# A three-group feed-forward stage: the first group's down products plain, the down weights' Strassen operands made in the second group

## The chip, the cores and the metric

One core of one Trainium2 chip. The metric is the device time of one execution, in microseconds (us), the median of several runs. The engines are TensorE (PE, with its weight loads as PEld), VectorE (DVE), ScalarE (ACT), GpSimd (POOL) and SyncE (SP, which here only issues DMAs). Each engine works through its own instructions in the order in which they were queued and waits on semaphores for the others.

## What is computed

One decoder layer for 2048 prompt tokens, 16 meta tokens and 8 x 4 sample tokens of width 1024: a mixer of three head groups, then a dense SwiGLU feed-forward network with hidden width 2816, then a norm. The change touches the feed-forward network alone:

```python
def _swiglu(hn, w_ffn_in, w_ffn_out):
    g, u = jnp.split(hn @ w_ffn_in, 2, axis=-1)
    return (jax.nn.silu(g) * u) @ w_ffn_out
...
        h = h + _swiglu(_rmsnorm(h, norm_ffn[l]), w_ffn_in[l], w_ffn_out[l])
...
    return _rmsnorm(h, norm_final), stacked
```

The outputs are float32. The kernel multiplies in float16, with each operand split into a high and a low half and three passes for each product (high x high, high x low, low x high; `PASSES`).

## The kernel before

The mixers fill the first 1034 us and are not touched. The feed-forward network then runs over three groups of token tiles, here called group 0, 1 and 2: the first two hold six tiles of 128 tokens, the last four tiles and the short tile 0. Tokens are paired, so that the matmuls of a group run over 384, 384 and 280 columns.

**Strassen.** Both products are made with seven products of blocks instead of eight (Winograd's form). For that each operand is needed as seven blocks: some as they are, four as sums. For a weight tile, `left` (gate and up weights, L1015 to L1018) and `right` (down weights, L1022 to L1025) make the four sums on POOL, and `operands` splits plain blocks and sums into high and low halves: ACT rounds to float16 (L155), DVE takes the rest (L156), in three pieces of 512, 256 and 1024 columns a tile.

**Hidden.** For each of 11 units `jq` of 256 hidden columns, `hidden` calls `quad` twice, for gate and up. Each `quad` makes seven products of 12 matmuls (L1239), combined on ACT, DVE and POOL; the POOL combinations L1248 and L1249 stand in the middle, and DVE's products with silu (L1262) need them. `put` then writes the down products' operands `hh`, high half by ACT (L1268) and low half by DVE (L1269): three blocks as they are, and four sums, which POOL makes first (L1274 to L1280).

**Down.** The units are taken in four parts of 2, 3, 3 and 3 (`PARTS`). After a part's hidden units, `down` runs for each half `m` of the output columns and each pair of tiles: seven products of 3 matmuls a unit with 256 columns (L1292), each summed over the part's units in PSUM, then combined and added to the residual rows `xr` (two ACT, eight DVE and three POOL instructions, L1302 to L1330).

**Weights.** Group 0 loads the raw weights (`raw`, six buffers), makes the operands of 44 gate and up tiles and 22 down tiles, and stores each tile of 896 KB in scratch memory (`kept`, tiles `w`, six buffers). Groups 1 and 2 load them back into eleven `w` buffers of a new pool, which is opened once, when group 1 begins. In parts 1 and 2 of group 0, `prep_late` also prepares x operands of later tiles, in the same buffers. Loads and stores are issued by SP in program order; the tile framework lets each wait for the last user of its buffer, and instructions of one engine stand in the order that the framework's scheduler gave them.

Of the kernel before, what the change touches and what calls it, by code (L numbers as in the profile page):

```python
# [17 lines left out]
P = 128  # L18
# [41 lines left out]
def trunk(ctx, tc, I, O, groups):  # L60
# [1049 lines left out]

    pg_cm = tc.tile_pool(name="pg", bufs=1, side="left", reuse_waits="tile")
    pg = [pg_cm.__enter__()]
    w_bufs = [6]

    def raw_tile():
        return pg[0].tile([P, 4, 256], F32, tag="raw", bufs=6, name=nm("raw"))

    def w_full():
        return pg[0].tile([P, 2, 7, 256], F16, tag="w", bufs=w_bufs[0], name=nm("w"))

    def w_tile():
        w = w_full()
# [2 lines left out]
    def sum_tile():  # L1125
        return pg[0].tile([P, 4, 256], F32, tag="sums", bufs=2, name=nm("sums"))

    def kept(dram, make):

        w = w_full()  # L1130
        parts = [w[:, 0], w[:, 1]]
        if w_bufs[0] == 6:
            make(parts)
            nc.sync.dma_start(dram, w.rearrange("p a o c -> p (a o c)"))
        else:
            nc.sync.dma_start(w.rearrange("p a o c -> p (a o c)"), dram)
        return parts
# [41 lines left out]
    def gu_operands(c0):  # L1179

        rows = w_gu[:, c0 : c0 + 256].rearrange("(h q k p) c -> q h p k c", h=2, q=2, p=P)

        def make(w, q):
            raw = raw_tile()
            for h in range(2):
                nc.sync.dma_start(raw[:, 2 * h : 2 * h + 2], rows[q, h])
            a = [[raw[:, 2 * h : 2 * h + 2, u * P : (u + 1) * P] for h in range(2)] for u in range(2)]
            left(w, sum_tile(), a[0][0], a[0][1], a[1][0], a[1][1], raw[:, :, 0:P], WG)

        return [kept(wgu_d[c0 % DFF // 256, c0 // DFF, q], lambda w: make(w, q)) for q in range(2)]  # L1190

    def dn_operands(jq, m):


        def make(w):
            raw = raw_tile()
            c = slice(m * 512, m * 512 + 512)
            nc.sync.dma_start(raw.rearrange("p (k h) c -> p k (h c)", k=2), w_dn[2 * jq * P : 2 * jq * P + 2 * P, c].rearrange("(k p) c -> p k c", p=P))
            right(w, sum_tile(), raw[:, 0], raw[:, 1], raw[:, 2], raw[:, 3], raw.rearrange("p (k h) c -> p h k c", k=2)[:, 0], WS)

        return kept(wdn_d[jq, m], make)

    gu_first = [gu_operands(c) for c in (0, DFF)]
    interleave(outs)
# [4 lines left out]
    with (  # L1209
# [45 lines left out]
        def hidden(q, jq, n):  # L1255
# [15 lines left out]
            put(A11, a11)  # L1271
            put(A12, a12)
            put(A22, a22)
            G.tensor_tensor(s1, a21, a22, op=ALU.add)  # L1274
            put(S1, s1)
            G.tensor_tensor(s2, s1, a11, op=ALU.subtract)
# [4 lines left out]
            put(S4, s4)  # L1281

        PRODS = ((A11, B11), (S2, T2), (S3, T3), (S1, T1), (A12, B21), (A22, T4), (S4, B22))

        def down(ws, x1, x2_, c, off, L):

# [57 lines left out]
        put_off = [pr for pr in all_pairs[early:] if pr[0]] + [[0]]  # L1344

        for gi, grp in enumerate(groups):
            if gi == 1:
                pg_cm.__exit__(None, None, None)
                pg_cm = tc.tile_pool(name="ph", bufs=1, side="left", reuse_waits="tile")
                pg[0] = pg_cm.__enter__()  # L1350
                w_bufs[0] = 11
            n = half[gi]

            rows2 = [[(pr[0], 0, P), (pr[1], 0, P)] if len(pr) == 2 else [(0, 0, T0 // 2), (0, T0 // 2, T0 // 2)] for pr in pairs(grp)]
# [6 lines left out]
            for q0, q1 in PARTS:  # L1361
# [8 lines left out]
                for m in range(2):  # L1370
                    c = slice(m * 512, m * 512 + 512)
                    ws = [dn_operands(jq, m) for jq in range(q0, q1)]
                    for ra, rb in rows2:
                        for _ in range(3):
                            next(ahead, None)
                        down(ws, xr[ra], xr[rb], c.start, offs[ra[0]][1], ra[2])
                        if final:
                            for rw in (ra, rb):
                                L = rw[2]
                                S.activation(ft2("junk", [P, D], F16)[:L, c], xr[rw][:L, c], AF.Square, accum_out=sq[rw][:L, m : m + 1])  # L1380
# [326 lines left out]
```

## Time and profile before

| what | value |
| --- | --- |
| median of 3 runs | 2410.7 us (2409.39 to 2413.79) |
| the profiled execution | 2401.93 us, its span 2399.9 us |
| mean granted clock of TensorE | 0.973 |
| group 0 on TensorE | 1034.64 to 1589.44 us of the span |
| group 1 | 1589.44 to 2043.36 us |
| group 2 and the end | 2043.36 to 2399.9 us |

The profiled execution lies 0.4% below the median. All views (windows, timeline, groups by line) are of this one execution, in us from the start of its span. Busy time of an engine that is off the critical path costs nothing in itself; what counts is which wait ends last before TensorE goes on.

### The profile page before, as it was taken

The numbers are of one execution on the slowest core, as the hardware profiler recorded it, in microseconds if no ns is written. First come the engines' busy times: TensorE is split into PE (matmuls) and PEld (weight loads), VectorE is DVE, ScalarE is ACT, GpSimd is POOL, SyncE is SP. The second block draws the span as 40 slices with busy tenths as digits, with TensorE's granted clock in tenths as the row PEclk, the third lists the DMA queues.
The fourth block names the chain that finished last, engine by engine and source line by source line (L and its number), as shares of the span: only waits on it lengthen the run. The fifth ranks groups of instructions, "written<-read, shape, count | busy, mean of one in ns | idle before, by whom it ended". The sixth has DMA issues, their size and how long they took to land. (4 is left out here: it accounts for less than half of the span.)

```text
span 2399.9 us, 51972 instructions
## 1 busy us (share of the span) xinstructions
PE 2215.4 (92%) x20298; PEld 1605.7 (67%) x20298; DVE 1673.4 (70%) x4064; ACT 941.8 (39%) x2526; POOL 1148.9 (48%) x1595
## 2 busy tenths in 40 slices
PE   6999999999999899787989979789999999999996
PEld 6677767767777445444657566567686867888886
DVE  8789888988988776558778687655454535655546
ACT  7455545545445432334343434422212122332323
POOL 7333233333333364559768787634332324544435
PEclk9999999999999999898999989999999999999998
DMA  7233333333323755995536545684334247744441
GB/s 259 46 67 70 67 74 62 75 65 80 66 65 83 188 192 181 304 305 193 188 140 216 190 169 203 178 305 174 123 121 157 108 168 194 272 176 172 181 166 39
DMA packets 294328, 364.95 MB, mean 152 GB/s; under 512 B 203807, under 2 KB 234479, under 8 KB 294066
## 3 DMA queue, kind: packets, MB, share of 16 engines
q1 hardware_dynamic: 285090, 331.02, 44.2%
q0 software_dynamic: 4384, 15.93, 1.7%
q10 hardware_dynamic: 4608, 14.68, 1.6%
q8 instruction: 159, 2.61, 0.4%
q14 instruction: 87, 0.71, 0.1%
HBM read 212.24 MB, written 103.50 MB: 132 GB/s over the span
## 5 line engine op out<-in xcount | busy, mean ns | idle before, releaser
L1239 PE MATMUL s<-x,w 128*128 128x384 f16 (+1 forms) x5544 | 827.8, 312 | 20.4 <-DMA w<-wgu_scratch 7.8
L1239 PEld LDWEIGHTS <-w 128*128 128x128 f16 x5544 | 543.2, 98 | 302.8 <-issue 19.0
L1292 PE MATMUL dn<-w,hh 128*128 128x256 f16 (+1 forms) x4158 | 446.6, 279 | 54.8 <-ACT hh L1268 21.8
L1292 PEld LDWEIGHTS <-hh 128*128 128x128 f16 (+1 forms) x4158 | 380.6, 99 | 119.6 <-issue 29.5
L212 PEld LDWEIGHTS <-xT 128*128 128x128 f16 (+1 forms) x1992 | 176.1, 99 | 188.6 <-issue 18.2
L1268 ACT ACTIVATE hh<-tmp 128x384 f16<-128x384 f32 (+1 forms) x231 | 112.4, 494 | 282.7 <-DVE tmp L1262 167.4
L1248 POOL TENSOR_TENSOR tmp<-tmp,tmp 128x384 f32<-128x384 f32 (+1 forms) x66 | 67.1, 1017 | 276.3 <-ACT tmp L1247 272.8
L1269 DVE TENSOR_TENSOR hh<-tmp,hh 128x384 f16<-128x384 f32 (+1 forms) x231 | 143.4, 628 | 75.7 <-ACT hh L1268 74.0
L212 PE MATMUL wo<-wo,xT 128*128 128x512 f16 x768 | 176.3, 387 | 7.6 <-DVE xn L992 3.0
L156 DVE SCALAR_TENSOR_TENSOR w<-raw,w 128x512 f16<-128x512 f32 (+1 forms) x136 | 108.5, 830 | 14.2 <-ACT w L155 14.2
L553 POOL TENSOR_TENSOR t<-t 128x8 f32<-128x8 f32 (+2 forms) x100 | 24.9, 249 | 188.2 <-DVE k L551 100.6
L1250 DVE TENSOR_TENSOR tmp<-s,tmp 128x384 f32<-128x384 f32 (+1 forms) x66 | 34.2, 519 | 108.4 <-PE s L1239 108.4
L212 PE MATMUL d<-xT,qf 128*128 128x128 f16 (+1 forms) x1632 | 107.4, 220 | 0.0
L156 DVE SCALAR_TENSOR_TENSOR w<-sums,w 128x1024 f16<-128x1024 f32 x68 | 98.5, 1450 | 9.5 <-ACT w L155 9.4
L1259 ACT ACTIVATE tmp<-tmp 128x384 f32<-128x384 f32 (+1 forms) x132 | 61.6, 490 | 109.0 <-DVE tmp L1250 51.7
L1324 DVE SCALAR_TENSOR_TENSOR xr<-dn,xr 128x256 f32<-128x256 f32 x192 | 78.9, 417 | 35.0 <-PE dn L1292 30.8
L212 PE MATMUL d<-xT,bqk 128*128 128x128 f16 (+1 forms) x1632 | 100.1, 220 | 3.3 <-DVE e L278 3.3
L212 PEld LDWEIGHTS <-qf 128*128 128x128 f16 x1632 | 95.2, 100 | 7.2 <-issue 2.1
L212 PEld LDWEIGHTS <-bqk 128*128 128x128 f16 x1632 | 93.0, 99 | 5.5 <-issue 4.6
L212 PE MATMUL d<-aig,xT 128*128 128x512 f16 (+1 forms) x408 | 92.7, 379 | 3.4 <-DVE g L358 3.4
L212 PE MATMUL d<-bvo,xT 128*128 128x512 f16 (+1 forms) x408 | 95.6, 380 | 0.2 <-DVE qlo L325 0.2
L212 PE MATMUL d<-xT,cq 128*128 128x128 f16 (+1 forms) x1632 | 94.8, 217 | 0.0
(536 smaller groups left out, 4044.2 us busy)
## 6 DMA issues: line engine op xcount, KB each, us to landing
w<-wgu_scratch SPq DMA_DIRECT2D x88, 896.0 KB
wgu_scratch<-w SPq DMA_DIRECT2D x44, 896.0 KB
w<-wdn_scratch SPq DMA_DIRECT2D x44, 896.0 KB
raw<-in_w_ffn_in_dram SPq DMA_DIRECT2D x88, 256.0 KB
wdn_scratch<-w SPq DMA_DIRECT2D x22, 896.0 KB
xs<-in_x_prompt_dram SPq DMA_DIRECT2D x26, 512.0 KB
x_scratch<-pT ACTq DMA_DIRECT2D x28, 448.0 KB
raw<-in_w_ffn_out_dram SPq DMA_DIRECT2D x22, 512.0 KB
```

What stands on the lines that cost most here:

```text
L156: V.scalar_tensor_tensor(lo, src, scale, hi, op0=ALU.mult, op1=ALU.subtract)
L212: T.matmul(out, lh(k, a), rh(k, b), start=(n == 0), stop=(n == 3 * nk - 1))
L553: G.tensor_tensor(tn, tv[:, :, :, 0], tv[:, :, :, 1], op=ALU.mult)
L1239: T.matmul(out, A[k // 2][p][:, a, k % 2 * P : k % 2 * P + P], x2[r][:, k // 2, op, k % 2, :n], start=i == 0, stop=i == 11)
L1248: G.tensor_tensor(r12, r12, r22, op=ALU.add)
L1250: V.tensor_tensor(r11, prod(A12, B21), r11, op=ALU.add)
L1259: S.activation(d, d, AF.Silu, scale=UF)
L1268: S.activation(hi, v, AF.Copy)
L1269: V.tensor_tensor(lo, v, hi, op=ALU.subtract)
L1292: T.matmul(out, hh[p][:, q, a, off : off + L], ws[q][r][:, b], start=(q, p, r) == order[0], stop=(q, p, r) == order[-1])
L1324: V.scalar_tensor_tensor(x[:L, cc], m, UD, x[:L, cc], op0=ALU.mult, op1=ALU.add)
```

## The change

Three things change. (1) In group 0 the down products are made plainly, by `down_plain`: from four blocks, each output block as six matmuls a unit (two halves k, three passes) with 512 columns, summed over the part's units, and one DVE instruction that adds the result to `xr`. `hidden` then puts four blocks of `hh` in place of seven, with the block A21 in the place of S1, and makes no sums. The down weights of group 0 are only split, one ACT and one DVE instruction of 1024 columns a tile. (2) The 22 down tiles' Strassen operands are made and stored by group 1 (the argument `when` of `kept`), which therefore loads raw down weights; group 2 loads the operands as before. (3) Each group now has a pool of its own: six raw and six w buffers in group 0, three and eight in group 1, eleven w buffers in group 2. `left`, `right`, `quad` and `down` are not altered.

```diff
-    w_bufs = [6]
+    stage, raw_bufs, w_bufs = [0], [6, 3], [6, 8, 11]
...
-    def kept(dram, make):
+    def kept(dram, make, when):
...
-        if w_bufs[0] == 6:
+        if stage[0] == when:
...
+        return [kept(wgu_d[c0 % DFF // 256, c0 // DFF, q], lambda w: make(w, q), 0) for q in range(2)]
...
-        return kept(wdn_d[jq, m], make)
+        if stage[0] == 0:
+            w = w_tile()
+            split_w(load().rearrange("p a c -> p (a c)"), *(z[:, 0:4].rearrange("p a c -> p (a c)") for z in w), WS)
+            return w
+        return kept(wdn_d[jq, m], make, 1)
...
             put(A22, a22)
+            if stage[0] == 0:
+                put(A21, a21)
+                return
...
+        def down_plain(ws, x1, x2_, c, off):
+
+            order = [(q, k, p, r) for q in range(len(ws)) for k in range(2) for p, r in PASSES]
+            for x, ops in ((x1, (A11, A12)), (x2_, (A21, A22))):
+                out = pbt("dn")
+                for o in order:
+                    q, k, p, r = o
+                    T.matmul(out, hh[p][:, q, ops[k], off : off + P], ws[q][r][:, 2 * k : 2 * k + 2].rearrange("p h c -> p (h c)"), start=o == order[0], stop=o == order[-1])
+                V.scalar_tensor_tensor(x[:, c : c + 512], out, UD, x[:, c : c + 512], op0=ALU.mult, op1=ALU.add)
...
-            if gi == 1:
+            if gi:
                 pg_cm.__exit__(None, None, None)
-                pg_cm = tc.tile_pool(name="ph", bufs=1, side="left", reuse_waits="tile")
+                pg_cm = tc.tile_pool(name=f"ph{gi}", bufs=1, side="left", reuse_waits="tile")
                 pg[0] = pg_cm.__enter__()
-                w_bufs[0] = 11
+                stage[0] = gi
...
-                        down(ws, xr[ra], xr[rb], c.start, offs[ra[0]][1], ra[2])
+                        if gi == 0:
+                            down_plain(ws, xr[ra], xr[rb], c.start, offs[ra[0]][1])
+                        else:
+                            down(ws, xr[ra], xr[rb], c.start, offs[ra[0]][1], ra[2])
```

How the order of instructions changes, at three places. First POOL ahead of the last hidden unit of group 0's last part. Before, the four-instruction sums of two down tiles (`sums` from `raw`) stand ahead of the last unit's up combination L1248:

```order
L1249 TENSOR_TENSOR tmp_21519<-tmp_21519,tmp_21518 128x384
L1022 TENSOR_TENSOR sums_22127<-raw_22125 128x256
L1024 TENSOR_TENSOR sums_22127<-raw_22125 128x256
L1023 TENSOR_TENSOR sums_22127<-raw_22125,sums_22127 128x256
L1022 TENSOR_TENSOR sums_22142<-raw_22140 128x256
L1024 TENSOR_TENSOR sums_22142<-raw_22140 128x256
L1025 TENSOR_TENSOR sums_22127<-raw_22125,sums_22127 128x256
L1023 TENSOR_TENSOR sums_22142<-raw_22140,sums_22142 128x256
L1025 TENSOR_TENSOR sums_22142<-raw_22140,sums_22142 128x256
L1248 TENSOR_TENSOR tmp_21657<-tmp_21657,tmp_21659 128x384
```

Now, in the same part (L1258 and L1259 are the former L1248 and L1249), the last gate and up sums stand ahead of the second of three units, and from there on the combinations follow each other:

```order
L1016 TENSOR_TENSOR sums_20592<-sums_20592,raw_20589 128x256
L1018 TENSOR_TENSOR sums_20592<-raw_20589,sums_20592 128x256
L1258 TENSOR_TENSOR tmp_20177<-tmp_20177,tmp_20179 128x384
L1259 TENSOR_TENSOR tmp_20179<-tmp_20179,tmp_20178 128x384
L1258 TENSOR_TENSOR tmp_20317<-tmp_20317,tmp_20319 128x384
L1259 TENSOR_TENSOR tmp_20319<-tmp_20319,tmp_20318 128x384
```

No sum stands ahead of the last unit there any more; in parts 1 and 3 of group 0, eight gate and up sums of the next part still do. The second place is POOL ahead of the last unit of group 1's second part. Before, the gate's and the up's combinations of a unit followed each other with no sums between:

```order
L1248 TENSOR_TENSOR tmp_23871<-tmp_23871,tmp_23873 128x384
L1249 TENSOR_TENSOR tmp_23873<-tmp_23873,tmp_23872 128x384
L1248 TENSOR_TENSOR tmp_23983<-tmp_23983,tmp_23985 128x384
L1249 TENSOR_TENSOR tmp_23985<-tmp_23985,tmp_23984 128x384
L1274 TENSOR_TENSOR tmp_23982<-tmp_23871,tmp_23873 128x384
```

Now the sums of two down tiles stand between them:

```order
L1259 TENSOR_TENSOR tmp_22521<-tmp_22521,tmp_22520 128x384
L1022 TENSOR_TENSOR sums_24097<-raw_24095 128x256
L1024 TENSOR_TENSOR sums_24097<-raw_24095 128x256
L1023 TENSOR_TENSOR sums_24097<-raw_24095,sums_24097 128x256
L1022 TENSOR_TENSOR sums_24112<-raw_24110 128x256
L1024 TENSOR_TENSOR sums_24112<-raw_24110 128x256
L1025 TENSOR_TENSOR sums_24097<-raw_24095,sums_24097 128x256
L1023 TENSOR_TENSOR sums_24112<-raw_24110,sums_24112 128x256
L1025 TENSOR_TENSOR sums_24112<-raw_24110,sums_24112 128x256
L1258 TENSOR_TENSOR tmp_22631<-tmp_22631,tmp_22633 128x384
```

The last unit's L1258 now follows eight sums. The third place is SP at the border between groups 1 and 2, where `w` are tiles of operands, `x` the group's inputs and `xr` its residual rows. Before, the first loads of group 2's gate weights follow the last down loads of group 1 and stand ahead of the inputs:

```order
L1136 DMA w_26920<-wdn_scratch 128x3584
L1136 DMA w_27250<-wgu_scratch 128x3584
L1136 DMA w_27252<-wgu_scratch 128x3584
L1136 DMA w_27362<-wgu_scratch 128x3584
L1057 DMA_TRANSPOSE x_2033_15774<-x_scratch 128x14x128
```

Now they follow group 1's last store, the inputs and the residual rows:

```order
L1057 DMA_TRANSPOSE x_2033_15774<-x_scratch 128x14x128 x2
L1068 DMA x_2032_15773<-x_scratch 128x28x24
L1068 DMA x_2033_15774<-x_scratch 128x28x24
L1392 DMA xr_26134<-h_scratch 24x1024
L1392 DMA xr_26132<-h_scratch 24x1024
L1138 DMA w_26136<-wgu_scratch 128x3584
L1138 DMA w_26138<-wgu_scratch 128x3584
```

The first load of group 2 belongs to the new pool and waits for the last down product of group 1.

More of the change, by code (lines that the diff above doesn't have):

```diff
@@ L1112, in trunk @@
     pg = [pg_cm.__enter__()]
-    w_bufs = [6]
+    stage, raw_bufs, w_bufs = [0], [6, 3], [6, 8, 11]
     def raw_tile():
-        return pg[0].tile([P, 4, 256], F32, tag="raw", bufs=6, name=nm("raw"))
+        return pg[0].tile([P, 4, 256], F32, tag="raw", bufs=raw_bufs[stage[0]], name=nm("raw"))
     def w_full():
-        return pg[0].tile([P, 2, 7, 256], F16, tag="w", bufs=w_bufs[0], name=nm("w"))
+        return pg[0].tile([P, 2, 7, 256], F16, tag="w", bufs=w_bufs[stage[0]], name=nm("w"))
     def w_tile():
@@ L1188, in make, with load @@
             left(w, sum_tile(), a[0][0], a[0][1], a[1][0], a[1][1], raw[:, :, 0:P], WG)
-        return [kept(wgu_d[c0 % DFF // 256, c0 // DFF, q], lambda w: make(w, q)) for q in range(2)]
+        return [kept(wgu_d[c0 % DFF // 256, c0 // DFF, q], lambda w: make(w, q), 0) for q in range(2)]
     def dn_operands(jq, m):
-        def make(w):
+        def load():
             raw = raw_tile()
@@ L1198, in make @@
             nc.sync.dma_start(raw.rearrange("p (k h) c -> p k (h c)", k=2), w_dn[2 * jq * P : 2 * jq * P + 2 * P, c].rearrange("(k p) c -> p k c", p=P))
+            return raw
+        def make(w):
+            raw = load()
             right(w, sum_tile(), raw[:, 0], raw[:, 1], raw[:, 2], raw[:, 3], raw.rearrange("p (k h) c -> p h k c", k=2)[:, 0], WS)
-        return kept(wdn_d[jq, m], make)
+        if stage[0] == 0:
[3 more added lines that the diff above has]
+        return kept(wdn_d[jq, m], make, 1)
     gu_first = [gu_operands(c) for c in (0, DFF)]
@@ L1283, in trunk @@
         PRODS = ((A11, B11), (S2, T2), (S3, T3), (S1, T1), (A12, B21), (A22, T4), (S4, B22))
+        A21 = S1
+        def down_plain(ws, x1, x2_, c, off):
[6 more added lines that the diff above has]
+                V.scalar_tensor_tensor(x[:, c : c + 512], out, UD, x[:, c : c + 512], op0=ALU.mult, op1=ALU.add)
         def down(ws, x1, x2_, c, off, L):
```

## Prediction

> **What bounds the kernel now.** First the page's span, then the view of windows, cut where the feed-forward part changes phase. Columns: window, length, busy us (and instructions) of PE, PEld, DVE, ACT, POOL, granted clock, DMA share, GB/s. The rows are group 0's first hidden stretch, its first down stretch, its rest, then groups 1 and 2.
>
> ```profile
> span 2399.9 us, 51972 instructions
> ```
>
> ```profile
> 1034.60:1098.90 64.30, 57.01 (x337) 33.48 (x336) 42.55 (x52) 27.22 (x49) 47.84 (x50) 0.95 0.87 290
> 1098.90:1154.80 55.90, 37.23 (x255) 26.86 (x253) 52.06 (x80) 20.34 (x42) 51.36 (x53) 0.76 0.54 198
> 1154.80:1589.40 434.60, 386.33 (x2656) 263.95 (x2653) 321.35 (x510) 176.31 (x355) 330.24 (x346) 0.95 0.54 183
> 1589.40:2043.40 454.00, 453.65 (x3235) 316.83 (x3236) 219.21 (x427) 107.45 (x233) 152.53 (x175) 1.00 0.47 167
> 2043.40:2399.90 356.50, 337.71 (x3236) 283.18 (x3233) 199.13 (x431) 110.38 (x281) 155.37 (x207) 0.98 0.45 169
> ```
>
> Groups 0 and 1 have the same columns and the same products. Group 1 takes 454.0 us, TensorE never idle; group 0 takes 554.8, with POOL busy 429 of them (153 in group 1) and DVE 416 (219): it makes the weights' operands. TensorE's timeline (start, length, engine, line, operation, names, shape, count, idle time before) gives the pace and the waits:
>
> ```profile
> 1041.75 2.08 PE L1239 MATMUL s<-x,w 128*128 128x384 f16 x6 [6.79 <-DMA x<-x_scratch]
> 1044.34 54.75 PE L1239 MATMUL s<-x,w 128*128 128x384 f16 x329 [0.51 <-DMA x<-x_scratch]
> 1098.93 0.49 PE L1292 MATMUL dn<-w,hh 128*128 128x256 f16 x3
> 1154.77 25.51 PE L1239 MATMUL s<-x,w 128*128 128x384 f16 x156
> 1236.76 0.70 PE L1158 MATMUL tr<-ident,raw 48*128 48x48 f32 x8
> 1254.72 17.77 PE L1292 MATMUL dn<-w,hh 128*128 128x256 f16 x146 [4.24 <-DVE xr L1324]
> 1298.00 74.26 PE L1239 MATMUL s<-x,w 128*128 128x384 f16 x456
> 1383.45 0.82 PE L1292 MATMUL dn<-w,hh 128*128 128x256 f16 x6
> 1441.86 58.34 PE L1239 MATMUL s<-x,w 128*128 128x384 f16 x358
> 1526.46 0.82 PE L1292 MATMUL dn<-w,hh 128*128 128x256 f16 x6
> 1533.55 1.04 PE L1292 MATMUL dn<-w,hh 128*128 128x256 f16 x4 [5.75 <-ACT hh L1268]
> 1546.49 35.11 PE L1292 MATMUL dn<-w,hh 128*128 128x256 f16 x316 [0.94 <-ACT hh L1268]
> 1589.44 56.41 PE L1239 MATMUL s<-x,w 128*128 128x384 f16 x336 [7.84 <-DMA w<-wgu_scratch]
> 1645.68 6.82 PE L1292 MATMUL dn<-w,hh 128*128 128x256 f16 x61
> ```
>
> ```profile
> 1755.77 41.43 PE L1292 MATMUL dn<-w,hh 128*128 128x256 f16 x378
> 1797.03 82.06 PE L1239 MATMUL s<-x,w 128*128 128x384 f16 x504
> 1878.93 41.43 PE L1292 MATMUL dn<-w,hh 128*128 128x256 f16 x378
> ```
>
> Start to start in group 1, 256 columns take (1797.03 - 1755.77) / 378 = 109.2 ns and 384 columns (1878.93 - 1797.03) / 504 = 162.5 ns. Group 0 has 1848 of the second (300.3 us) and 1386 of the first (151.4), 451.7 us; the other 103.1 of its 554.8 are waits and cold clock. Each stretch less its matmuls at these paces: hidden 1, 64.3 - 54.6 = 9.7 (7.3 of it waiting for x); down 1, 55.8 - 27.5 = 28.3; hidden 2, 0.1; down 2, 61.2 - 41.3 = 19.9; hidden 3, 3.6; down 3, 58.4 - 41.3 = 17.1; hidden 4, 2.7; down 4 (to 1581.60), 55.1 - 41.3 = 13.9; the change of group, 7.8.
>
> Why the downs wait shows on POOL, which works in order: part 4's last hidden unit, then the same place in group 1.
>
> ```profile
> 1527.53 1.10 POOL L1022 TENSOR_TENSOR sums<-raw 128x256 f32<-128x256 f32 x1 [1.80 <-DVE w L156]
> ...
> 1534.28 0.72 POOL L1025 TENSOR_TENSOR sums<-raw,sums 128x256 f32<-128x256 f32 x1
> 1534.96 0.99 POOL L1248 TENSOR_TENSOR tmp<-tmp,tmp 128x384 f32<-128x384 f32 x1
> ```
>
> ```profile
> 1750.75 0.99 POOL L1248 TENSOR_TENSOR tmp<-tmp,tmp 128x384 f32<-128x384 f32 x1 [11.64 <-ACT tmp L1247]
> ```
>
> Eight sums of down weights stand ahead of the combination L1248 that the last unit needs. It starts 8.5 us after the hidden products' end (1526.46); group 1 has it 5.0 us before (1755.77). DVE's products, the puts of hh and TensorE queue up behind it.
>
> **The change part by part.**
>
> *Plain downs on TensorE:* 792 matmuls of 512 columns replace 1386 of 256. The output projection has that width:
>
> ```profile
> 1019.80 8.58 PE L212 MATMUL wo<-wo,xT 128*128 128x512 f16 x39
> ```
>
> 8.58 us less a drain of 0.17 (41.43 - 41.26 above), over 39, is 215.6 ns; twice 109.2 is 218.4. I take 216.5: 792 x 0.2165 = 171.5, so **+20.1 us** (+19.4 to +21.6), all on the path, since nothing but TensorE is left to bound group 0 between its waits. The Trainium skill (TensorE: Matmul & The Clock Gate, Back-to-back issue gap) puts a sustained stream of 512-column matmuls at about 131 ns each; by that the term would be 792 x 0.131 - 151.4 = -48 us. The row above, 39 in a row at 215.6 ns, does not agree, and the measurement decides.
>
> *What leaves group 0.* The last row is the nearest to the new evictions of 128x512. Groups by line, 1030 to 1590 of before (count, busy us, mean ns, idle before):
>
> ```profile
> L1022 POOL TENSOR_TENSOR sums<-raw 128x256 f32<-128x256 f32 x22 | 25.1, 1143 | 25.2 <-DVE w L156 25.2
> L1274 POOL TENSOR_TENSOR tmp<-tmp,tmp 128x384 f32<-128x384 f32 x11 | 14.3, 1298 | 17.2 <-DVE tmp L1262 17.2
> L1326 POOL TENSOR_TENSOR tmp<-tmp,tmp 128x256 f32<-128x256 f32 x24 | 20.2, 841 | 7.9 <-ACT tmp L1305 6.4 <-DVE tmp L1304 1.3 <-ACT junk L1380 0.2
> L1269 DVE TENSOR_TENSOR hh<-tmp,hh 128x384 f16<-128x384 f32 x77 | 51.5, 673 | 41.0 <-ACT hh L1268 40.7
> L156 DVE SCALAR_TENSOR_TENSOR w<-sums,w 128x1024 f16<-128x1024 f32 x64 | 92.6, 1448 | 6.1 <-ACT w L155 6.0
> L156 DVE SCALAR_TENSOR_TENSOR w<-raw,w 128x512 f16<-128x512 f32 x64 | 58.1, 907 | 13.7 <-ACT w L155 13.6
> L156 DVE SCALAR_TENSOR_TENSOR w<-raw,w 128x256 f16<-128x256 f32 x64 | 47.2, 737 | 0.0
> L1324 DVE SCALAR_TENSOR_TENSOR xr<-dn,xr 128x256 f32<-128x256 f32 x72 | 29.1, 413 | 4.9 <-PE dn L1292 4.3
> L998 DVE SCALAR_TENSOR_TENSOR xs<-wo,xs 128x512 f32<-128x512 f32 x3 | 2.1, 688 | 4.1 <-PE wo L212 3.1 <-DMA xs<-in_x_prompt_dram 1.1
> ```
>
> POOL loses 88 sums of down weights (at 1.1 us, 97), 44 sums for hh (at 1.3, 57) and 72 combinations (at 0.84, 61): half of its 429. DVE loses 33 puts (22), 22 of each narrow split (36; one of 1024 wide per tile stays) and, per down, eight instructions of at least 0.41 for two of 0.69 (24 x 1.9 = 46): a quarter of its 416. ACT loses three puts and two narrow splits likewise. None of this is itself on the path; what counts is the waits behind it:
>
> - Down 4 and down 3: in the new order no down sums stand ahead of the last unit (in part 3 eight gate sums do, with their inputs loaded early). The first 12 to 15 plain matmuls of a part (2.6 to 3.2 us) need only the first units, and four puts follow instead of seven. I leave 2 us each of 13.9 and 17.1 (0.5 to 5).
> - Down 1: eight gate sums still stand ahead of the last unit, at 0.7 to 1.2 us each, 6 to 9 us, and some wait for buffers; the cover is 2 to 3. I leave 7 of 28.3 (3 to 14).
> - Down 2: the wait of 4.24 there is for DVE's evictions, which stand behind splits. Four splits of 1.45 remain ahead of the last put, beside the small tile's preparation (row L1158). I leave 5.7 of 19.9 (2.7 to 13).
> - Hidden 1 and 2 stay at 9.8; hidden 3 and 4 wait for the units' combinations, also behind sums: 2 of 6.3 left (0.5 to 5).
> - The change to group 1: loads wait for the last use of the released buffers. They were issued at 1581.31 and landed 8.1 later:
>
> ```profile
> 1581.31 5.58 SPq L1136 DMA_DIRECT2D w<-wgu_scratch x8
> 2021.24 4.24 SPq L1136 DMA_DIRECT2D w<-wgu_scratch x5
> ```
>
> The buffer they wait for is now last read six plain matmuls (1.3 us) before the end, not three narrow ones (0.3): 6.8 of 7.8 left (6 to 8).
>
> Left: 9.8 + 7 + 5.7 + 2 + 2 + 2 + 6.8 = 35.3, so 67.8 of the waits go; with +20.1, group 0: **-47.7**.
>
> *What comes to group 1:* 22 tiles at four POOL sums (88, at 0.7 to 1.1 us: 60 to 100) and splits on DVE of 0.74 + 0.91 + 1.45 = 3.1 us (68). POOL goes from 153 to some 241 of 454 us, DVE from 219 to 287. Cover is there on average, not everywhere: in the new order, in two of the four parts, eight sums of the next tiles stand ahead of the last unit's L1248, which has 5.0 us to spare (row 1750.75), and eight at 0.72 to 1.1 take 6 to 9. I take 1.5 each, **+3** (0 to +12). Loads of 22 tiles turn into loads of raw weights and stores; the DMA share of 0.47 has room.
>
> *The new border between groups 1 and 2.* Row 2021.24: in before, group 2's weights were on their way 22 us ahead. Now its buffers belong to a new pool, and the first load waits for the last down product of group 1. So the 8.1 us from issue to landing are bare, and group 2 starts cold: at the other border the first stretch took 1645.68 - 1589.44 = 56.2 us for 54.6 of matmuls, 1.6 more. **+9.8** (+6 to +12). SP works in order too: behind the waiting load stand all of group 2's other loads, and TensorE waits for the first of them; ahead of it stand loads of x and of residual rows, which wait for the last hidden products and for group 1's output and so go earlier.
>
> Sum: -47.7 + 3 + 9.8 = **-34.9 us**. The profiled execution took 2401.9 (span 2399.9 and 2 around it), giving 2367; the median of the three runs shown is 2410.7, 0.4% above, giving **2376**, which I forecast. A difference under 0.2% (4.8 us) can't be told from none.
>
> **The rivals.**
>
> *Group 0 stays bound by the gate operands* (chance 0.18): its POOL and DVE still make 40 gate tiles, and half of the waits of downs and hidden 3 and 4 (85.5 in all) stay, 43 instead of 18.7: -47.7 + 24 + 12.8 = -11, 2400. For it: down 2's wait is DVE's. Against: POOL loses half its work.
>
> *The waits move with the operands, and the kernel is slower* (0.07). If group 1's four last units wait behind sums as group 0's part 3 and 4 did (13.9 and 17.1), that is 62 us instead of 3: -47.7 + 62 + 9.8 = +24, 2435. It decides from 9.5 us a part. For it: eight sums in the same place, all the S sums still on POOL, and eight w buffers instead of eleven. Against: POOL at 53% where group 0 had 77%, no gate sums beside the down sums, and TensorE 5.0 us behind L1248 to begin with. The Trainium skill (SBUF — State Buffer, Who interferes with whom) has a rule against this change: a DVE instruction with two SBUF inputs and a POOL instruction that reads SBUF exclude each other for their whole length. By it, POOL's 241 us in group 1 and DVE's new splits and puts (68 + 77 x 0.673 = 120) could not overlap; that fills 361 of 454 us, so the average still fits and only the places just named can lose. The trace agrees in so far as the same kind of sum takes 0.72 us (1534.28) and 1.14 on average (L1022).
>
> *The downs become clean* (0.15), since puts and splits thin out together: no waits but 9.8 + 2 + 6.8 in group 0: -103.1 + 18.6 + 20.1 = -64.4, and with 9.8 at the new border -55, 2356.
>
> *The border costs double* (0.08), if the first load lands only behind the stores of group 1's last operands and the residual rows: another 8.1 us, 2384. Against: by the order the stores stand ahead of the loads of x, and those wait for hidden products that end 41 us before the border.
>
> **How the numbers follow.** The forecast has 0.52. Its own bounds and the clean case reach down to 2356, the first rival up to about 2405: range 2356 to 2404. Faster by over 0.2%: forecast, clean, border, and two thirds of the first rival, 0.87; same 0.05; slower 0.08.
>
> **What would show it.** TensorE's timeline: 512-column downs at 0.216 us; waits ahead of downs 3 and 4 under 5 us; down 1 the longest left; 8 us with a DMA of w ahead of group 2, where none was. Wrong: L1258 (the new L1248) in group 1 later than the end of its products, or group 0 over 520 us.

## The result, and the profile after

| kernel | median us | ratio to before, 95% interval |
| --- | --- | --- |
| before | 2410.05 | 1 |
| changed | 2367.95 | 0.9836 [0.9811, 0.9862] |
| changed, measured again beside other kernels | 2364.0 | 0.9827 [0.9805, 0.9849] |

The change takes 42.1 us off; 34.9 were forecast. The profiled execution went from a span of 2399.9 to 2356.9 us, 43.0 less. The total came out by two errors of opposite sign: group 0 gained more than forecast, group 1 lost more. One execution of the last kernel of the experiments (no borders) took 4568.02 us; its ratio leaves it out, its median of six runs does not.

The view of windows of the changed kernel, columns as before; the rows are groups 0, 1 and 2 with the end:

```profile
1039.35:1520.53 481.18, 474.05 (x2650) 259.13 (x2648) 287.16 (x421) 174.60 (x319) 221.10 (x244) 0.99 0.55 184
1520.53:1998.67 478.14, 460.54 (x3234) 318.34 (x3235) 277.63 (x497) 144.53 (x301) 244.34 (x265) 0.98 0.48 168
1998.67:2356.90 358.23, 339.43 (x3234) 283.88 (x3234) 195.37 (x423) 109.97 (x279) 152.19 (x202) 0.98 0.48 185
```

Group 0 takes 481.2 us instead of 554.8 (-73.6), but begins 4.7 later, because the output projection ahead of it ended later. Group 1 takes 478.1 instead of 453.9 (+24.2), group 2 and the end 358.2 instead of 356.5 (+1.7): -73.6 + 4.7 + 24.2 + 1.7 = -43.0. POOL's busy time in group 0 fell from 429 to 221 us, and in group 1 it rose from 153 to 244, just what was worked out (half, and 241).

TensorE's timeline of the changed kernel (L1249 the hidden products, L1307 the plain downs, L1317 the Strassen downs):

```profile
1039.35 54.76 PE L1249 MATMUL s<-x,w 128*128 128x384 f16 x336
1093.95 2.54 PE L1307 MATMUL dn<-w,hh 128*128 128x512 f16 x11
1096.76 28.88 PE L1307 MATMUL dn<-w,hh 128*128 128x512 f16 x133 [0.27 <-DVE hh L1279]
1125.47 82.06 PE L1249 MATMUL s<-x,w 128*128 128x384 f16 x504
1207.47 0.69 PE L1160 MATMUL tr<-ident,raw 48*128 48x48 f32 x8
1209.65 48.47 PE L1307 MATMUL dn<-w,hh 128*128 128x512 f16 x216 [1.49 <-ACT w L155]
...
1339.86 46.78 PE L1307 MATMUL dn<-w,hh 128*128 128x512 f16 x216
1386.47 82.06 PE L1249 MATMUL s<-x,w 128*128 128x384 f16 x504
1468.38 46.78 PE L1307 MATMUL dn<-w,hh 128*128 128x512 f16 x216
```

Downs 3 and 4 have no wait left. Down 1 is 31.5 us long for 144 matmuls of 0.2165 (31.2), down 2 (with the eight transposes) is 3.7 longer than its 46.8. The pace of 512 columns: (1386.47 - 1339.86) / 216 = 215.8 ns.

```profile
1520.53 56.87 PE L1249 MATMUL s<-x,w 128*128 128x384 f16 x336 [5.37 <-DMA w<-wgu_scratch]
1577.24 0.93 PE L1317 MATMUL dn<-w,hh 128*128 128x256 f16 x7
...
1583.11 5.30 PE L1317 MATMUL dn<-w,hh 128*128 128x256 f16 x33 [3.98 <-DVE hh L1279]
...
1612.55 82.06 PE L1249 MATMUL s<-x,w 128*128 128x384 f16 x504
1694.45 1.36 PE L1317 MATMUL dn<-w,hh 128*128 128x256 f16 x11
1699.19 41.92 PE L1317 MATMUL dn<-w,hh 128*128 128x256 f16 x367 [3.38 <-DVE hh L1279]
1740.95 82.06 PE L1249 MATMUL s<-x,w 128*128 128x384 f16 x504
...
1827.59 41.92 PE L1317 MATMUL dn<-w,hh 128*128 128x256 f16 x367 [3.38 <-DVE hh L1279]
...
1998.67 41.88 PE L1249 MATMUL s<-x,w 128*128 128x280 f16 x336 [4.74 <-DMA w<-wgu_scratch]
```

Group 1's downs now wait where they had not: down 1 takes 35.3 us (28.2 in before, 1645.68 to 1673.87), downs 2 and 3 take 46.5 (41.3), down 4 takes 1.4 more. In downs 2 and 3 the wait is 3.4 us, and the 367 matmuls behind it take 41.76 from start to start (1699.19 to 1740.95) instead of 367 x 0.1092 = 40.1: 1.7 us come on top of each wait. That is slow clock: the granted clock was 0.96 in this stretch, and 1.00 in the same down of before. At the new border the wait is 4.7; SP issued the load when the last down ended (1993.63), and TensorE went on 5.0 us later:

```profile
1993.63 4.77 SPq L1138 DMA_DIRECT2D w<-wgu_scratch  x8
```

POOL at the end of group 1's second part shows the wait's root:

```profile
1688.56 1.11 POOL L1022 TENSOR_TENSOR sums<-raw 128x256 f32<-128x256 f32 x1 [1.80 <-DVE w L156]
...
1695.33 0.72 POOL L1025 TENSOR_TENSOR sums<-raw,sums 128x256 f32<-128x256 f32 x1
1696.02 0.99 POOL L1258 TENSOR_TENSOR tmp<-tmp,tmp 128x384 f32<-128x384 f32 x1
```

It is the picture that before showed in group 0: eight sums, held up by a split on DVE, and the last unit's combination starts 1.6 us after the hidden products' end (1694.45), where before it had started 5.0 us ahead of it. That is one of the two signs by which the prediction said that it would be wrong.

### The profile page after: what moved, and what is told of

It reads as the page before. It is cut to its first block, busy times and chain, and to the rows that moved or that the text cites. A ratio compares the mean times of both kernels' runs of the same rounds, so it can differ in the third digit from the quotient of the medians.

```text
span 2356.9 us, 50351 instructions
## 1 busy us (share of the span) xinstructions
PE 2221.3 (94%) x19704; PEld 1544.2 (66%) x19704; DVE 1600.5 (68%) x3909; ACT 928.4 (39%) x2467; POOL 1028.4 (44%) x1479
## 5 line engine op out<-in xcount | busy, mean ns | idle before, releaser
L1249 PE MATMUL s<-x,w 128*128 128x384 f16 (+1 forms) x5544 | 826.6, 312 | 10.1 <-DMA w<-wgu_scratch 10.1
L1249 PEld LDWEIGHTS <-w 128*128 128x128 f16 x5544 | 543.5, 98 | 292.0 <-DMA w<-wgu_scratch 10.9
L212 PEld LDWEIGHTS <-xT 128*128 128x128 f16 (+1 forms) x1992 | 177.1, 99 | 191.3 <-issue 24.2
L1317 PE MATMUL dn<-w,hh 128*128 128x256 f16 (+1 forms) x2772 | 276.3, 275 | 13.5 <-DVE hh L1279 12.3
L1317 PEld LDWEIGHTS <-hh 128*128 128x128 f16 (+1 forms) x2772 | 239.5, 98 | 49.5 <-DVE hh L1279 14.9
L1278 ACT ACTIVATE hh<-tmp 128x384 f16<-128x384 f32 (+1 forms) x198 | 95.5, 488 | 226.7 <-DVE tmp L1272 157.6
L1258 POOL TENSOR_TENSOR tmp<-tmp,tmp 128x384 f32<-128x384 f32 (+1 forms) x66 | 64.7, 980 | 264.5 <-ACT tmp L1257 231.3
L1307 PE MATMUL dn<-w,hh 128*128 128x512 f16 x792 | 173.5, 382 | 1.8 <-ACT w L155 1.5
L1279 DVE TENSOR_TENSOR hh<-tmp,hh 128x384 f16<-128x384 f32 (+1 forms) x198 | 115.7, 591 | 51.3 <-ACT hh L1278 50.0
L1307 PEld LDWEIGHTS <-hh 128*128 128x128 f16 x792 | 77.8, 98 | 96.2 <-issue 3.6
L156 DVE SCALAR_TENSOR_TENSOR w<-raw,w 128x512 f16<-128x512 f32 (+2 forms) x158 | 122.3, 802 | 25.6 <-ACT w L155 25.5
L155 ACT ACTIVATE w<-raw 128x512 f16<-128x512 f32 (+2 forms) x158 | 84.7, 583 | 98.6 <-PE dn L1307 63.0
L1260 DVE TENSOR_TENSOR tmp<-s,tmp 128x384 f32<-128x384 f32 (+1 forms) x66 | 34.2, 518 | 104.9 <-PE s L1249 104.8
L1015 POOL TENSOR_TENSOR sums<-raw 128x256 f32<-128x256 f32 x44 | 50.2, 1140 | 113.8 <-DVE w L156 113.6
```

The source lines that it names most:

```text
L155: S.activation(hi, src, AF.Copy, scale=scale)
L156: V.scalar_tensor_tensor(lo, src, scale, hi, op0=ALU.mult, op1=ALU.subtract)
L212: T.matmul(out, lh(k, a), rh(k, b), start=(n == 0), stop=(n == 3 * nk - 1))
L1249: T.matmul(out, A[k // 2][p][:, a, k % 2 * P : k % 2 * P + P], x2[r][:, k // 2, op, k % 2, :n], start=i == 0, stop=i == 11)
L1258: G.tensor_tensor(r12, r12, r22, op=ALU.add)
L1260: V.tensor_tensor(r11, prod(A12, B21), r11, op=ALU.add)
```

## The experiments

The theory going in: sums of down weights, by their place in POOL's queue ahead of the last hidden unit, cause the waits, in group 0 before and in group 1 now. The rivals: the amount of work on POOL and DVE, wherever it is queued; and the lighter product form (fewer puts, sums and combinations). Times within the feed-forward part are compared by the lengths of groups, since the mixers ahead of it ended between 1034 and 1053 us from one profiled execution to the next. These lengths, read from one execution each, have a spread of their own: two profiles of the changed kernel have 481.2 and 486.9 us for group 0, from the wait for x, the clock in the first hidden stretch and the wait at the border; their downs' waits differ by under 0.5 us. "Waits in downs" is the sum over group 0's four downs of their length less their matmuls, as in the prediction: 79.2 us in before, 4.0 in the changed kernel. Each ratio is to runs of before on the same chip. The medians come from several chips. These share one: plain downs alone, move alone, changed with sums held back and changed with one pool; the changed kernel measured again, both, both with the second half, and no borders; the two kernels of before with sums held back, and seven puts. Cells that no argument uses are left empty.

| kernel | median us | ratio | group 0 | waits in its downs | group 1 |
| --- | --- | --- | --- | --- | --- |
| before | | 1 | 554.8 | 79.2 | 453.9 |
| changed | | 0.9836 | 481.2 | 4.0 | 478.1 |
| plain downs alone | 2367.73 | 0.9851 [0.9822, 0.988] | 512.9 | 25.7 | 454.8 |
| move alone | 2374.31 | 0.9871 [0.9849, 0.9893] | 495.0 | 29.6 | 478.3 |
| before without down sums | 2375.48 | 0.9849 [0.9826, 0.9872] | 514.7 | 52.9 | |
| before, sums held back | 2402.39 | 0.9979 [0.9961, 0.9997] | 542.4 | 64.7 | |
| before, held back, no border | 2393.06 | 0.9945 [0.9925, 0.9966] | 532.9 | | |
| changed, seven puts | 2376.6 | 0.987 [0.9843, 0.9898] | 489.6 | 3.6 | |
| changed, sums held back | 2362.99 | 0.9828 [0.9807, 0.9849] | 484.7 | | 468.8 |
| changed, one pool | 2362.35 | 0.9821 [0.9798, 0.9844] | 483.6 | | 473.0 |
| changed, both | 2350.36 | 0.9768 [0.9746, 0.979] | 482.3 | | 463.6 |
| changed, both, second half too | 2351.96 | 0.9774 [0.9752, 0.9797] | 485.1 | | 463.4 |
| changed, held back, no borders | 2348.05 | 0.976 [0.974, 0.9781] | 482.8 | | 458.8 |

**Plain downs alone**, and **the move alone**: the two halves of the change. The first also has the buffers and the one new pool of before; the second keeps those of the change.

```diff
-        if stage[0] == 0:
-            w = w_tile()
...
-        return kept(wdn_d[jq, m], make, 1)
+        return kept(wdn_d[jq, m], make, 0)
```

> The plain downs alone: group 0 still makes and stores the down weights' Strassen operands and groups 1 and 2 load them into eleven buffers, as in before; the plain products of group 0 read four of the seven stored blocks, so its sums are not the reference's. Theory (sums of down weights queued on POOL ahead of the last hidden unit cause most of group 0's waits): POOL loses 118 of 429 us but not those sums, so downs 1 to 4 keep about 15, 12, 8 and 8 us of 79, the border 8; group 0 about 535 us, groups 1 and 2 as in before: 2390 us (2380 to 2400), some 22 above the changed kernel. Rival (the lighter product form, four puts and no combinations, is what removes the waits): group 0 about 486 us as in the changed kernel, and no loss in group 1 or at its end: 2343 us.

```diff
-            if stage[0] == 0:
-                put(A21, a21)
-                return
...
                 a, b = PRODS[i]
+                b = b % 4 if stage[0] == 0 else b
...
-                        if gi == 0:
-                            down_plain(ws, xr[ra], xr[rb], c.start, offs[ra[0]][1])
-                        else:
-                            down(ws, xr[ra], xr[rb], c.start, offs[ra[0]][1], ra[2])
+                        down(ws, xr[ra], xr[rb], c.start, offs[ra[0]][1], ra[2])
```

> The move alone: group 0 keeps the seven Strassen products, seven puts and all their combinations, but its down weights are only split and its products read the four split blocks in place of seven, so its sums are not the reference's; group 1 makes and stores the operands. Theory: without the down sums on POOL the downs of group 0 lose most of their waits (15 to 25 us of 103 left beside the 8 of the border), and TensorE saves the 20 us of the plain products: group 0 about 485 us, group 1 24 us longer and group 2 2 longer as in the changed kernel: 2368 us (2355 to 2385). Rival (the puts, hh sums and combinations cause the waits): group 0 stays over 535 us, 2415 us.

Plain downs alone gave a median of 2367.73 us and a ratio of 0.9851, not told apart from the whole change (0.9836). That lies outside the theory's 2380 to 2400, and short of the rival's 2343. Its TensorE timeline in group 0:

```profile
1127.01 3.59 PE L1303 MATMUL dn<-w,hh 128*128 128x512 f16 x8 [6.53 <-ACT hh L1274]
...
1379.53 45.46 PE L1303 MATMUL dn<-w,hh 128*128 128x512 f16 x202 [3.98 <-DVE hh L1275]
...
1514.04 46.65 PE L1303 MATMUL dn<-w,hh 128*128 128x512 f16 x202 [3.99 <-DVE hh L1275]
```

The eight down sums are still there (in part 4 the last unit's combination starts at 1510.87, 4.1 us after the products' end at 1506.73), but the plain products lose 7.2 us there (a wait of 4.0, and a granted clock of 0.94 behind it) where the Strassen ones lost 13.9: 25.7 us of waits in the four downs.

The move alone leaves 29.6 us of waits in the downs, where the theory left 15 to 25 in all of group 0 beside the border; most are in down 1 and down 2:

```profile
1102.67 0.93 PE L1315 MATMUL dn<-w,hh 128*128 128x256 f16 x7
...
1146.26 82.06 PE L1249 MATMUL s<-x,w 128*128 128x384 f16 x504
1228.26 0.70 PE L1160 MATMUL tr<-ident,raw 48*128 48x48 f32 x8
...
1277.59 82.06 PE L1249 MATMUL s<-x,w 128*128 128x384 f16 x504
```

That is 43.6 - 27.5 = 16.1 and 49.3 - 41.3 = 8.0 us. This kernel does not pay the 20 us of the plain products, but it pays the 24 of group 1. Group 1 is as long as the changed kernel's (478.3 and 478.1), so that loss belongs to the move and not to the plain form; with the plain downs alone it is 454.8. The two halves by themselves take 53.5 and 49.6 us out of 79.2; together they can take no more than what there is, and took 75.2.

**The sums' place in the queue**, tried in before, without touching any work:

```diff
-            right(w, sum_tile(), raw[:, 0], raw[:, 1], raw[:, 2], raw[:, 3], raw.rearrange("p (k h) c -> p h k c", k=2)[:, 0], WS)
+            with tc.issue_after(behind[0]) if m else nullcontext():
+                right(w, sum_tile(), raw[:, 0], raw[:, 1], raw[:, 2], raw[:, 3], raw.rearrange("p (k h) c -> p h k c", k=2)[:, 0], WS)
...
-            G.tensor_tensor(s4, a12, s2, op=ALU.subtract)
+            last = G.tensor_tensor(s4, a12, s2, op=ALU.subtract).ins
             put(S4, s4)
+            behind[0] = last
```

> The kernel before with one ordering edge: POOL's sums for the second half's down tiles (m = 1) are queued behind the last hidden unit of their part, so that none of them stands ahead of its L1248. Theory (much of group 0's waits is the place in POOL's queue, not the amount of work): downs 3 and 4 fall from 31 to about 8 us of waits, downs 1 and 2 from 48 to about 37, hidden 3 and 4 from 6 to 3: 37 us, 2369 us, nearly all of what the change brought. Rival (the amount of work on POOL and DVE, which stays, causes the waits): they move to the second half's operands and the time stays within 10 us of 2406.

The theory fell here: 0.9979, where 0.985 was expected; the rival had the time within 10 us of before. On POOL, in part 4 (L1250 is the former L1248), no sum stands ahead of the last unit's combination any more, and it still starts late:

```profile
1533.39 0.99 POOL L1250 TENSOR_TENSOR tmp<-tmp,tmp 128x384 f32<-128x384 f32 x1 [6.60 <-DVE tmp L1248]
```

It starts 3.0 us after the hidden products' end (1530.35) instead of 8.5, because DVE is late as well: five splits of w, from 1528.55 to 1532.12, stand ahead of the eviction that it waits for (L1248 is a DVE instruction in this kernel, at 1532.69). And the sums that were held back are then late for the second half. TensorE, down 3 and the second half of it:

```profile
1392.46 1.04 PE L1295 MATMUL dn<-w,hh 128*128 128x256 f16 x4 [3.71 <-ACT hh L1270]
...
1421.02 8.60 PE L1295 MATMUL dn<-w,hh 128*128 128x256 f16 x62 [2.72 <-ACT w L155]
```

The waits in downs fall by 14.5 us to 64.7, and those in hidden 2 to 4 rise from 6.4 to 18.6. So in group 0 it is not POOL's queue alone: with the sums out of the way, the splits on DVE stand ahead of the same unit, and what was held back is late elsewhere.

The same with one pool for all groups asks what the border costs in before (raw six to four, w to seven buffers, no pool opened for group 1):

```diff
-        return pg[0].tile([P, 4, 256], F32, tag="raw", bufs=6, name=nm("raw"))
+        return pg[0].tile([P, 4, 256], F32, tag="raw", bufs=4, name=nm("raw"))
...
-        return pg[0].tile([P, 2, 7, 256], F16, tag="w", bufs=w_bufs[0], name=nm("w"))
+        return pg[0].tile([P, 2, 7, 256], F16, tag="w", bufs=7, name=nm("w"))
...
-                pg_cm.__exit__(None, None, None)
-                pg_cm = tc.tile_pool(name="ph", bufs=1, side="left", reuse_waits="tile")
-                pg[0] = pg_cm.__enter__()
```

> The same, and a single pool for all groups (four raw and seven w buffers), so that group 1's first weights need not wait for the last down product of group 0. Theory: the 7.8 us of that wait and 1.6 of cold matmuls go too: 9 us less than with the edge alone. Rival (four raw buffers instead of six hold back group 0's sums): equal to the edge alone or slower.

9.3 us less (2402.39 to 2393.06), as expected.

**Whose work, POOL's or DVE's and ACT's.** The kernel before without the 88 sums of down weights in group 0, all splits kept:

```diff
-            right(w, sum_tile(), raw[:, 0], raw[:, 1], raw[:, 2], raw[:, 3], raw.rearrange("p (k h) c -> p h k c", k=2)[:, 0], WS)
+            operands(w, raw.rearrange("p (k h) c -> p h k c", k=2)[:, 0], raw[:, 3].unsqueeze(1), raw, WS)
```

> The kernel before without the 88 POOL sums of down weights: the splits on ACT and DVE stay as many and as wide, and read the raw blocks where they read the sums, so the stored operands are not Strassen's and the sums of all groups are not the reference's. It leaves out 96 of POOL's 429 us in group 0 and nothing of DVE's. If POOL is what group 0's downs wait for, whatever the place in the queue, their waits fall from 79 to 30 as with the move alone: 50 us, 2356 us. If it is the DVE and ACT work of the splits as much, they fall by less than 20 us: 2388 us or more.

It lies between: 33 us less, the waits in downs at 52.9. TensorE in down 1 and down 3:

```profile
1114.51 5.18 PE L1292 MATMUL dn<-w,hh 128*128 128x256 f16 x31 [7.55 <-ACT hh L1268]
...
1380.11 1.04 PE L1292 MATMUL dn<-w,hh 128*128 128x256 f16 x4 [4.94 <-ACT hh L1268]
```

The windows from down 1's end to group 1's start, of this kernel and then of the move alone (which lacks the same sums, and 44 narrow splits on each of ACT and DVE besides):

```profile
1154.61:1563.13 408.52, 380.93 (x2657) 261.09 (x2654) 310.36 (x510) 176.18 (x355) 266.80 (x275) 0.97 0.59 195
```

```profile
1146.26:1535.04 388.78, 374.74 (x2657) 259.32 (x2654) 293.44 (x472) 161.89 (x319) 258.26 (x272) 0.99 0.50 161
```

POOL has nearly the same work in both (267 and 258 us); DVE has 17 us less and ACT 14 less in the second, and the waits in downs are 29.6 instead of 52.9. Of the 49.6 us that the move takes out, 26.3 go with POOL's sums. The other 23.3 go with the splits, or with the loads and stores, which differ between these two kernels too (195 and 161 GB/s); these were not tried by themselves.

**Fewer puts.** The changed kernel with the seven puts and the four sums of hh back in group 0:

```diff
                 put(A21, a21)
-                return
...
-            put(S1, s1)
+            if stage[0]:
+                put(S1, s1)
```

> The changed kernel with the four sums of hh and all seven puts back in group 0 (the three more are written and not read; the output is unchanged). If fewer puts and sums for hh are what the plain form brings, the downs of group 0 go from 4 us of waits to 15 or more, towards the 30 of the move alone: 2378 us. If it is that the plain products need only the first four puts and begin with 12 to 15 matmuls of the earlier units, the sums and puts behind them cost little: 2368 us, downs at 4 to 8.

TensorE's downs 1, 3 and 4 of group 0:

```profile
1113.33 2.54 PE L1307 MATMUL dn<-w,hh 128*128 128x512 f16 x11
1117.00 28.88 PE L1307 MATMUL dn<-w,hh 128*128 128x512 f16 x133 [1.13 <-DVE hh L1279]
...
1358.74 46.78 PE L1307 MATMUL dn<-w,hh 128*128 128x512 f16 x216
...
1487.26 46.78 PE L1307 MATMUL dn<-w,hh 128*128 128x512 f16 x216
```

The waits in downs are 3.6 us, as without them: fewer puts and sums are not what the plain form brings, once the down operands are made elsewhere. What in the plain form by itself took out 53.5 us (the combinations and evictions that it does without, or that it begins with 11 to 14 matmuls of 512 columns which need only the earlier units) was not separated.

This kernel also bears on the amount of work. In group 0 it has POOL busy for 285 us and DVE for 316, and the changed kernel 221 and 287: more work, no more wait in the downs. Plain downs alone has 310 and 320, little more than this one, and 25.7 us of waits. The sums and puts for hh of a part's last unit come behind what the plain products need first; the eight down sums of plain downs alone stand ahead of that unit. So with plain downs it is what stands ahead that costs, more than the amount.

The median, though, is 2376.6, near what was expected of the other alternative, and its interval touches the changed kernel's (0.987 [0.9843, 0.9898] and 0.9827 [0.9805, 0.9849]). In the profiled execution the excess of group 0 lies ahead of the downs, in a wait for x at the start (5.8 us) and a late end of the mixers (1050.02). Whether the seven puts cost something there stays open.

**Group 1's loss.** Its POOL has room (244 of 478 us). The changed kernel with the next part's sums queued behind the last hidden unit of the part before:

```diff
-            right(w, sum_tile(), raw[:, 0], raw[:, 1], raw[:, 2], raw[:, 3], raw.rearrange("p (k h) c -> p h k c", k=2)[:, 0], WS)
+            with tc.issue_after(behind[0]) if behind[0] is not None else nullcontext():
+                right(w, sum_tile(), raw[:, 0], raw[:, 1], raw[:, 2], raw[:, 3], raw.rearrange("p (k h) c -> p h k c", k=2)[:, 0], WS)
...
             put(S4, s4)
+            behind[1] = last
...
             for q0, q1 in PARTS:
+                behind[0] = behind[1]
```

> The changed kernel with one ordering edge more: in group 1, POOL's sums for a part's down weights are queued behind the last hidden unit of the part before. Theory (the place in POOL's queue is what costs: eight sums of the next part's tiles ahead of the last L1258): waits of group 1's first three downs, 17.5 us, fall to about 3, so 2353 us (2349 to 2358). Rival (the added load on POOL, DVE and their contention is what costs): the same work is there, 2368 us, within 4.

TensorE, down 2 of group 1, and then POOL and DVE ahead of it (L1260 is the former L1248, L1258 its supplier on DVE):

```profile
1704.53 8.79 PE L1320 MATMUL dn<-w,hh 128*128 128x256 f16 x75
1714.20 33.38 PE L1320 MATMUL dn<-w,hh 128*128 128x256 f16 x303 [0.87 <-DVE hh L1281]
```

```profile
1701.94 0.99 POOL L1260 TENSOR_TENSOR tmp<-tmp,tmp 128x384 f32<-128x384 f32 x1 [5.07 <-DVE tmp L1258]
```

```profile
1697.37 1.22 DVE L156 SCALAR_TENSOR_TENSOR w<-sums,w 128x1024 f16<-128x1024 f32 x1
...
1699.44 1.22 DVE L156 SCALAR_TENSOR_TENSOR w<-sums,w 128x1024 f16<-128x1024 f32 x1
...
1701.23 0.56 DVE L1258 TENSOR_TENSOR tmp<-s,tmp 128x384 f32<-128x384 f32 x1
```

Here the place does count: L1260 now starts 2.6 us ahead of the products' end (1704.53) instead of 1.6 behind it, the wait of 3.4 us shrinks to 0.9, and group 1 gets 9.3 us shorter (478.1 to 468.8). It was to be 14.5: POOL now waits for DVE, whose splits stand ahead of its own evictions. In the medians the edge alone can't be told from nothing (0.9828 beside 0.9836); beside one pool it can, below.

**The borders.** One pool for groups 1 and 2, three raw and eight w buffers:

```diff
-    stage, raw_bufs, w_bufs = [0], [6, 3], [6, 8, 11]
+    stage, raw_bufs, w_bufs = [0], [6, 3, 3], [6, 8, 8]
...
             if gi:
+                stage[0] = gi
+            if gi == 1:
                 pg_cm.__exit__(None, None, None)
```

> The changed kernel with one pool for groups 1 and 2 (three raw, eight w buffers), so that group 2's first weights need not wait for the last down product of group 1. Theory: the wait of 4.7 us with a DMA and the cold first matmuls (1.7) go: 2362 us (2358 to 2366). Rival (eight w buffers are too few for group 2, which takes a w tile in less time with 280 columns): group 2 waits for w in several places, 2368 us or more.

Group 2 starts without a wait and at full clock:

```profile
2004.55 40.20 PE L1249 MATMUL s<-x,w 128*128 128x280 f16 x336
```

Groups 1 and 2 up to the last down take 779.5 us (1531.51 to 2311.01) instead of 786.3 (1520.53 to 2306.81): 6.8 less, 6.4 had been reckoned, and eight buffers are enough. The median, 2362.35, is near the 2362 that was expected, though by its ratio (0.9821) it is not told apart from the changed kernel's. The edge and the one pool together, then the second half's sums held back too (`behind[m]` for `behind[0]`), then one pool for all three groups with the edge (`raw_bufs, w_bufs = [4, 4, 4], [7, 7, 7]`, no pool opened in between), with the changed kernel once more beside them:

> The changed kernel once more, beside the next three: 0.983 to 0.984 of the kernel before, as measured first.

> The changed kernel with the ordering edge for the next part's sums in group 1 and one pool (three raw, eight w buffers) for groups 1 and 2. In their traces the edge took 9 us out of group 1 and the one pool 6.7 out of groups 1 and 2. If they act in different places, as the theory has it, they add: 16 us, 0.977 of before. Rival (one hides the other, since the weights' loads come earlier into the same buffers): no better than the one pool alone, 0.982.

> As the one with edge and one pool, and the sums for the second half's tiles also queued behind the last hidden unit of their own part. Theory (each sum ahead of a unit's combinations costs): group 1's remaining 10 us of waits fall to about 4, 0.974 to 0.975 of before. Rival (these operands are then late for the second half's downs, 20.6 us after the hidden products, with three tiles to make at 4 us of POOL and 3 of DVE each, and the DVE also evicts): 0.977 to 0.982.

> The changed kernel with the ordering edge and a single pool for all three groups, four raw and seven w buffers, so that neither border opens a new pool. Theory: both waits with a DMA of w (5.4 and 4.7) and the cold matmuls behind them (1.6 each) go beside the edge's 9: 22 us, 0.974. Rival (four raw buffers starve the making of gate operands in group 0, or seven w buffers group 2): waits with raw or w inside the groups, 0.98 or more.

Edge and pool add, as expected: 0.9768, 13.6 us below the changed kernel on the same chip (2364.0 to 2350.36), and 2.3% below before. Holding back the second half's sums as well only moves the wait: the first half of the down runs through, and the second half's first product waits for its weights.

```profile
1700.71 22.43 PE L1320 MATMUL dn<-w,hh 128*128 128x256 f16 x204
1725.03 19.31 PE L1320 MATMUL dn<-w,hh 128*128 128x256 f16 x174 [1.89 <-ACT w L155]
```

No border at all has the lowest ratio, 0.976 (0.974 was expected), though not told apart from 0.9768. The wait with a DMA at group 1's start is gone, but with four raw buffers down 1 of group 0 waits 6.0 us again, so group 0 is as long as with the border (482.8 and 482.3). There POOL's gate sums ahead of the last unit wait for loads of raw weights (1.0 and 1.8 us, from 1094.21 on), which they did not with six buffers, and eleven of them, not eight, stand ahead:

```profile
1107.14 1.25 PE L1310 MATMUL dn<-w,hh 128*128 128x512 f16 x5 [2.21 <-ACT hh L1280]
1112.17 30.48 PE L1310 MATMUL dn<-w,hh 128*128 128x512 f16 x132 [3.78 <-DVE hh L1281]
...
1530.15 54.76 PE L1251 MATMUL s<-x,w 128*128 128x384 f16 x336
```

## Why the prediction was right, and where not

The total is near the forecast partly by luck. Group 0 gained 73.6 us instead of 47.7, and 9.7 of the 73.6 are a wait that is not put down to the change (hidden 1, below); group 1 lost 19 instead of 3.

- *Plain downs, +20.1 us.* Right: 792 matmuls at 215.8 ns are 170.9 us, +19.5. By the 131 ns a matmul that the prediction quotes from the Trainium skill (TensorE: Matmul & The Clock Gate, Back-to-back issue gap) and gave up for the row of the output projection, the term would have missed by 67 us.
- *Waits that leave group 0's downs.* 16.7 us were to stay, 4.0 did. The step that failed is down 1: eight gate sums ahead of the last unit were priced at 7 us of wait and cost 0.3. On POOL, from the first of the eight to the combination behind them:

```profile
1083.51 0.73 POOL L1017 TENSOR_TENSOR sums<-raw 128x256 f32<-128x256 f32 x1
...
1093.26 1.31 POOL L1258 TENSOR_TENSOR tmp<-tmp,tmp 128x384 f32<-128x384 f32 x1
```

The sums were not cheaper than thought, 9.8 us for 6 to 9. But POOL came to them 10.4 us before the hidden products ended (1093.95), so L1258 was 0.7 ahead of that end, and the first 11 plain matmuls (2.5 us) covered all but 0.3 of the rest. The forecast counted the sums' length and not when POOL is free to begin them. Down 2 was the longest left and not down 1 (5.7 forecast, 3.7 measured, 1.7 of it clock): the splits and the transposes, as named. Downs 3 and 4 went to nothing instead of 2 each, hidden 3 and 4 likewise.
- *Why they leave.* The mechanism as told (the sums' place ahead of L1248) was a part of it. Held back by themselves they gave 3 us in the medians (0.9979); left out, 33; with 44 splits on each of ACT and DVE gone too (and other loads and stores), the waits in downs fell to 29.6. So POOL's sums are not all of it. The seven puts, work of the same engines behind what the products need, cost no wait in the downs. That it is the instructions ahead of the last unit on all three engines fits these runs; no run moved the splits by themselves, so this is not shown.
- *Hidden 1, 9.7 us kept.* It vanished in the profiled execution (1039.35 to 1093.95 is 54.6), but the part also began 4.7 us later; in the second profile of the same kernel the wait for x was 2.1 and the granted clock behind it 0.97. Over all profiles here that wait goes from 0 to 7.3 us. That is how the end of the mixers and the loads of x happen to fall, and not the change, as far as these profiles tell; 5.0 of the 43 us lie there.
- *Group 1, +3 (0 to +12).* Wrong, by its own working: 19 us without the border, outside its bounds. The place was named rightly (eight sums ahead of L1248, in parts 2 and 3), and the sums' price too: 7.5 us, from 1688.56, after a split on DVE had let go of their buffer, made L1258 6.6 us later than in before, within the 6 to 9. The step that failed is the 5.0 us to spare, which was counted whole. L1258 is not the last thing that TensorE needs: L1259 and two DVE instructions follow, the last of them this put:

```profile
1698.59 0.55 DVE L1279 TENSOR_TENSOR hh<-tmp,hh 128x384 f16<-128x384 f32 x1
```

From L1258's start (1696.02) to TensorE's going on (1699.19) it took 3.2 us, and the 11 matmuls ahead of the wait covered 1.4 of them. So L1258 had to start 1.8 us ahead of the products' end, 3.2 of the 5.0 could be spent, and 6.6 later is a wait of 3.4. Each such wait brought 1.7 of slow clock with it, so that a part cost 5.2 in place of 1.5. Part 1, with two units only, lost 7.1 and had been counted at nothing. The rival with the waits moved to group 1 was thus a third true: it needed 9.5 us a part to turn the sign, and got 4.7 on average.
- *The new border, +9.8.* The wait came where it was said, at 4.7 + 1.7 = 6.4: TensorE went on 5.0 us after the first load's issue (1993.63), not 8.1. The one pool confirms the price: 6.8 us less.

## What to carry to other kernels

When an operand is made once and used in several stages, look for a stage where the side engines have room, and then look at which of its instructions the schedule puts ahead of the ones that the main engine waits for, and at what still follows those: a combination that starts ahead of the main engine's need has less to spare than it seems. In group 1, with POOL busy for half of the time, an ordering edge won back 9.3 of 19 us; in group 0 of before, with 77%, it mostly moved the wait. Two ways to lighten a full stage do not add: either half of this change took two thirds of the same waits, and most of the gain was there without the other. The new pool between groups 1 and 2 exposed the first load's latency, and one pool for both hid it.

## What the runs showed of the hardware

A short wait can cost as much again in clock. In down 2 of group 0, the same 1.49 us wait behind eight small transposes is followed by 216 matmuls in 48.47 us in the changed kernel and in 46.78 with one pool (granted clock 0.96 and 1.00):

```profile
1222.14 46.78 PE L1307 MATMUL dn<-w,hh 128*128 128x512 f16 x216 [1.49 <-ACT w L155]
```

Behind the 3.38 us waits of group 1 it was 1.7 us in both parts, at a granted clock of 0.96. The Trainium skill (TensorE: Matmul & The Clock Gate, What's actually happening) has a free-running window of about 3.4 us, and half the clock after an idle window until a busy one: an estimate from that is 1.7 us for each time. The 1.7 us here agree with it, and a window that runs freely would fit that the same wait is charged in one execution and not in the next. No run here shows the window itself, and the waits that were charged, 1.49 and 3.38 us, are shorter than it.

Behind a border, TensorE went on 5.0 us after the issue of the first load of 896 KB in one place (1993.63) and 8.1 in another (1581.31), and the wait at the border of groups 0 and 1 went from 5.2 to 7.8 us over the kernels that have it.
